# Scaling the even output weight by the gate earlier in the program and keeping the result in DRAM

## The chip, the cores and the metric

The kernel runs on one core of a Trainium2 chip. The metric is the device time of one execution in microseconds (us), as the median of several runs. The engines are named as in the profile: PE is TensorE, DVE is VectorE, ACT is ScalarE, POOL is GpSimd, SP is the engine that issues most DMAs.

## What is computed

Two layers over 1024 tokens of 1024 channels. The even layer runs gated linear attention (GLA, four heads) and multi-head latent attention (MLA, eight heads) in parallel, puts their outputs side by side, multiplies by an output weight, scales each output channel with a gate and adds the result to the residual before a layer norm. The odd layer mixes with a Fourier transform and a gated MLP and ends in the same way.

```python
y_lat = jnp.einsum('bne,ed->bnd', jnp.concatenate([y_gla, y_mla], -1), w_out)   # even layer, w_out 1024 x 1024
x = layer_norm(DEEPNORM_ALPHA * x + gate[:, None, :] * y_lat, post_ln_g[l], post_ln_b[l])
```

The gate multiplies output channels, so it may be multiplied into the columns of the output weight beforehand. `gate` depends on the conditioning vector alone and is known long before the weight is used.

## The kernel before

All arithmetic is float32. A product of two operands is made of three matmuls (`mm3`, lines 143 to 148): each operand is split into a rounded part `hi` (an ACT cast, line 136) and the remainder `lo` (a DVE or POOL subtraction, line 141).

Nearly all large tiles, 128 x 1024 words, come from one pool `big` of 48 buffers through `b4`; tiles of 128 x 512 come from a pool `work` of 8 buffers through `w2`. The tile framework gives out the buffers of a pool in the order in which the program asks for them, sets every semaphore, and fixes the order of each engine's instructions when the program is built, by readiness and then by place in the program. On the chip each engine runs its list in that order.

The order in which the program asks is written by hand with generators: `weave` (line 51) runs several generators side by side, each in proportion to a total that is given with it. The stretch that matters first is woven of three streams: `in_proj_b` (ten projections of 128 columns, the last four of which multiply the GLA outputs by a gate), a chain of `gla` and `mla_ramp`, and the rest of the modulation. `mla_ramp` (line 873) loads and splits the MLA weights, normalised queries and keys, makes the queries and keys of head 0, moves them into place (`mla_prep`, line 978; a row of maxima joins the query tile `qh` by a small POOL DMA of `mr`), and last takes four gate tiles `mg` from DRAM, applies SiLU and writes them back (lines 905 to 909). `mla` (line 1012) then makes the values `V`, and runs eight heads; `attend(hd)` (line 1041) loads a gate tile `mg` for each pair of heads (line 1045), and for each of 20 blocks makes scores `pss`, takes exponentials `pexp` (ACT), splits them into `ph` (ACT cast; the subtraction alternates between DVE and POOL) and multiplies by `V` into `psav`, five blocks behind.

Beside heads 6 and 7 runs `even_pre` (line 1116): it loads the gate of the even layer as a row repeated over 128 partitions (`rowB`), and four row blocks of the output weight (`out_weight`, line 1136: SP load into `owr`, POOL multiplication by the gate, split into `hi` and `lo`). The other four row blocks follow in `rest` of `even_tail` (line 1204), behind the first half of the output projection of three row blocks (`out_proj`, line 1152). The odd layer calls `out_weight` in the same way with its own weight and gate.

Of the kernel before, what the change touches and what calls it, by code (L numbers as in the profile page):

```python
# [63 lines left out]
def chain(*gens):  # L64
    for g in gens:
        yield from g
# [6 lines left out]
def scaled(gen, f):  # L73
    for d in gen:
        yield d * f


def run(g):
    for _ in g:
        pass  # L80
# [1035 lines left out]
def even_pre(k):  # L1116

    nc, A = k.nc, k.A
    k.ow, k.oy = [None] * KD, [[None] * KD, [None] * KD]
    k.ogate = load_rows(k, k.gate[0])  # L1120
    for t in range(4):
        out_weight(k, A["wo0"], t)
        yield 2.5
    yt = []
    for t in range(4):
        x = k.b4(name="yg")
        nc.sync.dma_start(x, k.ygd[t])
        k.D("yg%d" % t, x)
        yt.append(x)
        if t % 2:  # L1130
            split_y(k, yt, t - 1)
            yt = []
        yield 2.5


def out_weight(k, wsrc, j):

    raw = k.b4(name="owr")
    k.nc.sync.dma_start(raw, wsrc[j * P:(j + 1) * P, :])
    k.nc.gpsimd.tensor_tensor(out=raw, in0=raw, in1=k.ogate, op=ALU.mult)  # L1140
    k.ow[j] = k.split(raw, (P, 1024))


# [54 lines left out]
def load_rows(k, src):  # L1198
    t = k.b4(name="rowB")
    k.nc.sync.dma_start(t, src.broadcast_to([P, D]))  # L1200
    return t


def even_tail(k, W):
    nc, A = k.nc, k.A
    k.x1 = [k.dr.tile([P, D], F32, name=f"x1_{i}") for i in range(NT)]

    def rest():
        for t in range(4, KD):
            out_weight(k, A["wo0"], t)  # L1210
        for t in range(0, 4, 2):
            k.D("ym%d" % t, k.mg[t])
            k.D("ym%d" % (t + 1), k.mg[t + 1])
            split_y(k, k.mg[t:t + 2], 4 + t)

    def resid(i):
        x = k.b4(name="xr")
        nc.sync.dma_start(x, A["x"][i * P:(i + 1) * P, :])
        return x

    pend = {}

    def done(i, x, c):
        nc.gpsimd.dma_start(k.x1[i], x)
        k.D("x1_%d" % i, x)
        r, nm = k.ln_stats(x)
        pend[i] = k.b4(name="xn1")
        nc.scalar.activation(out=pend[i], in_=x, func=AF.Identity, scale=r, bias=nm)

    k.h1 = [[], []]  # L1230

    def transposed(hf):
        for j in range(KD):
            if j % 2 == 0:
                hi, lo = k.b4(F32R, (P, 2, 512), name="h1h"), k.b4(F32R, (P, 2, 512), name="h1l")
            ps = k.bank()
            for t in range(4):
                nc.tensor.transpose(ps[:, t * P:(t + 1) * P], pend[4 * hf + t][:, j * P:(j + 1) * P], k.ident)
            hh = k.w2(name="h1")
            nc.scalar.activation(out=hh, in_=ps, func=AF.Identity, scale=k.s1[:, j:j + 1], bias=k.sh1[:, j:j + 1])  # L1240
            k.h1[hf].append(k.split(hh, None, hi=hi[:, j % 2, :], lo=lo[:, j % 2, :], hi_eng="dve"))
            yield 0.65

    first = transposed(0)
    for n, _ in enumerate(out_proj(k, list(range(KD)), rest, 0, resid, done), 1):
        if n in TR0:
            run(itertools.islice(first, TR0[n]))
        if n == WN:
            W.fill(WF)
    return transposed(1)  # L1250
# [41 lines left out]
def odd(k, transposed, W):  # L1292
    nc, A = k.nc, k.A
    T = nc.tensor

    f = [k.b4(F32, (P, 2, 512), name="f") for _ in range(NT // 2)]
    wf = []

    def wnext(c):
        if c == len(wf):  # L1300
            wf.append(W.next())
        return wf[c]

    ev = lambda i, ps: nc.scalar.copy(out=f[i // 2][:, i % 2, :], in_=ps)
    run(weave((natural_steps(k, wnext, 0, ev), 20.8), (chain(lull(TR1[0]), transposed), TR1[0] + TR1[1])))
    odd_consts(k)
    run(natural_steps(k, wnext, 1, ev))
    del wf[:]
    W.fill(2)
    UR, UI = butterflies(k, f)  # L1310
    del f
    X, fr = {}, []

    def dft(stage, g):
        if stage == 0:
            X[g] = dft_tokens(k, [z and z[:, g * P:(g + 1) * P] for z in UR], [z and z[:, g * P:(g + 1) * P] for z in UI])
        else:
            fr.append(dft_channels(k, X.pop(g)))
            k.D("fr%d" % g, fr[-1])


    wv = [W.next() for _ in range(KD // 2)]
    vg = [k.b4(F32, (P, 2, 512), name="vg") for _ in range(NT // 2)]
    mv = k.cpool.tile([P, NT * 4, 2], F32, name="vmv")
    for i in range(NT):
        ps = k.bank()
        o = slice((i % 4) * P, (i % 4) * P + P)
        for kk in range(KD):
            hh = k.h1[i // 4][kk]
            k.mm3(ps, (hh[0][:, o], hh[1][:, o]), (wv[kk // 2][0][:, kk % 2, :], wv[kk // 2][1][:, kk % 2, :]), kk == 0, kk == KD - 1)  # L1330
        for z in DFT.get(i, ()):
            dft(*z)
        v = vg[i // 2][:, i % 2, :]
        k.act(v, ps, AF.Gelu)
        st = k.sm.tile([P, 4, 6], F32, tag="vst", name="vst")
        for g in range(4):
            nc.vector.bn_stats(out=st[:, g, :], in_=v[:, g * P:(g + 1) * P])
            nc.vector.bn_aggr(out=mv[:, i * 4 + g, :], in_=st[:, g, :])
    rs = k.cpool.tile([P, NT * 4], F32, name="vrs")
    for i in range(0, NT, 4):  # L1340
        c = slice(i * 4, i * 4 + 16)
        nc.gpsimd.tensor_scalar(out=rs[:, c], in0=mv[:, c, 1], scalar1=EPS, scalar2=0.0, op0=ALU.add, op1=ALU.add)
        nc.gpsimd.tensor_tensor(out=rs[:, c], in0=rs[:, c], in1=k.mhalf[:, 0:16], op=ALU.pow)
    for i in range(NT):
        for g in range(4):
            c = i * 4 + g
            v = vg[i // 2][:, i % 2, g * P:(g + 1) * P]
            nc.vector.tensor_scalar(out=v, in0=v, scalar1=mv[:, c, 0:1], scalar2=rs[:, c:c + 1], op0=ALU.subtract, op1=ALU.mult)

    gu = []  # L1350
    for t in range(4):
        w = W.next()
        x = k.b4(name="gu")
        proj1(k, w, lambda ps, s: k.act(x[:, s:s + 512], ps, AF.Gelu))
        gu.append(x)

    for t in range(4):
        w = W.next()

        def ev(ps, s):  # L1360
            g = k.w2(name="gs")
            k.act(g, ps, AF.Silu)
            nc.vector.tensor_tensor(out=gu[t][:, s:s + 512], in0=gu[t][:, s:s + 512], in1=g, op=ALU.mult)

        proj1(k, w, ev)
        for s in range(2):
            ps = k.bank("pssgu")
            for c in range(4):
                i = 4 * s + c
                T.matmul(ps[:, c * P:(c + 1) * P], vg[i // 2][:, i % 2, t * P:(t + 1) * P], k.sguw[:, t, :], start=True, stop=True)  # L1370
            sv = k.w2(name="sv")
            bb = k.sgub[:, t:t + 1, :].broadcast_to([P, 4, P])
            nc.vector.tensor_tensor(out=sv.rearrange("p (c x) -> p c x", x=P), in0=ps.rearrange("p (c x) -> p c x", x=P), in1=bb, op=ALU.add)
            o = slice(s * 512, s * 512 + 512)
            nc.vector.tensor_tensor(out=gu[t][:, o], in0=gu[t][:, o], in1=sv, op=ALU.mult)

    k.ow, k.oy = [None] * KD, [[None] * KD, [None] * KD]
    k.ogate = load_rows(k, k.gate[1])
    for t in range(4):
        if t % 2 == 0:  # L1380
            split_y(k, gu[t:t + 2], 4 + t)
        w = W.next()
        out_weight(k, A["wo1"], 4 + t)

        def ev(ps, s):
            g = k.w2(name="gs")
            k.act(g, ps, AF.Silu)
            nc.vector.tensor_tensor(out=fr[t][:, s:s + 512], in0=fr[t][:, s:s + 512], in1=g, op=ALU.mult)

        proj1(k, w, ev)  # L1390
    return fr, gu
# [87 lines left out]
def odd_tail(k, fr):  # L1479
    nc, A = k.nc, k.A  # L1480

    def rest():
        for t in range(4):
            if t % 2 == 0:
                split_y(k, fr[t:t + 2], t)
            out_weight(k, A["wo1"], t)

    def resid(i):
        x = k.b4(name="xr")
        nc.sync.dma_start(x, k.x1[i])  # L1490
        return x

    run(out_proj(k, [4, 5, 6, 7, 0, 1, 2, 3], rest, 1, resid, lambda i, x, c: nc.sync.dma_start(k.out[i * P:(i + 1) * P, c], x[:, c])))
# [3 lines left out]
def hybrid(ctx: ExitStack, tc, A, out, dbg=None):  # L1497
# [11 lines left out]
    h, first = startup(k, context)  # L1509
    ada = ada_rest(k)  # L1510
    in_proj_a(k, h, hc, first, context, W, ada)
    run(weave((in_proj_b(k, h, W), 103.0), (chain(gla(k), scaled(mla_ramp(k), RAMP)), GLA_T + RAMP * 30), (ada, ADA_T)))
    mla(k)
    W = Weights(k, odd_weights(k))
    transposed = even_tail(k, W)
# [98 lines left out]
```

## Time and profile before

| | us |
|---|---|
| median of 3 runs (1150.33 to 1151.75) | 1150.7 |
| the profiled execution, its own time | 1151.5 |
| span of its trace | 1149.0 |
| PE busy | 1093.9 |
| DVE busy | 746.2 |
| ACT busy | 562.7 |
| POOL busy | 261.0 |

The profile is one execution. An engine is busy while it runs an instruction; matmuls are pipelined, so their durations overlap. The granted clock of PE is given as a mean share of full speed. "Idle before" stands in brackets with what ended it. A timeline row merges neighbouring instructions of one line and one tile (x4).

### The profile page before, as it was taken

Reading aid. Unit: us, or ns where it says so; the run is one execution under the profiler, and the core shown is the slowest. Engines: PE = TensorE matmul, PEld = TensorE weight load, DVE = VectorE, ACT = ScalarE, POOL = GpSimd, SP = SyncE. Lnnn points to the kernel's source line nnn. Section 1 sums busy time; section 2 is a strip of 40 time slices with the busy share of each in tenths; the row PEclk is TensorE's granted clock in tenths of the full one; section 3 lists DMA queues with packets and bytes.
Section 4 is the critical chain, followed back from the end, with each engine's and each line's share of the span. In section 5 each row is a group of like instructions: output and inputs, shape, how many; then the busy total and the mean of one; then the engine's idle time right before and its main releaser. Section 6 shows DMA issues by size and latency. Waiting matters only on the chain.

```text
span 1149.0 us, 14553 instructions
## 1 busy us (share of the span) xinstructions
PE 1093.9 (95%) x5288; PEld 868.1 (76%) x5288; DVE 746.2 (65%) x1264; ACT 562.7 (49%) x965; POOL 261.0 (23%) x260
## 2 busy tenths in 40 slices
PE   5889999899999999999999999999999999999997
PEld 3668778688687877767677666888788888888885
DVE  6867694866655675766777677798526633664544
ACT  6285655676562367857777778313422223332000
POOL 3520000000000023433324366343101000122111
PEclk8989999999999999999999999999999999999999
DMA  9635562333535752113302424333400311125111
GB/s 371 244 127 193 205 223 100 135 123 106 197 101 190 227 158 51 27 43 88 70 1 51 124 73 132 126 111 128 165 1 1 110 37 55 56 65 213 53 55 55
DMA packets 41752, 131.89 MB, mean 115 GB/s; under 512 B 5673, under 2 KB 7465, under 8 KB 41682
## 3 DMA queue, kind: packets, MB, share of 16 engines
q1 hardware_dynamic: 35578, 114.77, 30.9%
q0 software_dynamic: 3312, 10.26, 2.2%
q10 hardware_dynamic: 2792, 5.94, 1.3%
q8 instruction: 41, 0.67, 0.2%
q14 instruction: 29, 0.24, 0.1%
HBM read 98.37 MB, written 20.36 MB: 103 GB/s over the span
## 4 chain that ended last, share of the span: by engine, by line
PE 76%; DVE 8%; ACT 6%; issue 3%; POOL 3%; DMA 3%; SPq 0%; POOLq 0%; DVEq 0%; ACTq 0%
PE ps L146 11%; PE ps L148 10%; PE ps L147 10%; PE pso L147 5%; PE pso L146 5%; PE pso L148 5%; PE psm L998 3%; PE pss L1073 3%; PE pss L1074 3%; PE pss L1075 3%; PE psav L1059 2%; PE psav L1057 2%; PE psav L1058 2%; PE psn L146 1%; PE psn L148 1%
## 5 line engine op out<-in xcount | busy, mean ns | idle before, releaser
L141 POOL TENSOR_TENSOR ph<-pexp,ph 128x512 fp32r<-128x512 f32 x80 | 108.3, 1358 | 170.3 <-ACT ph L136 150.4
L118 ACT ACTIVATE pexp<-pss 128x512 f32<-128x512 f32 x160 | 93.3, 596 | 63.8 <-PE pss L1075 60.9
L999 DVE TENSOR_REDUCE mx<-psm 128x1 f32<-128x512 f32 (+1 forms) x192 | 102.2, 593 | 14.1 <-PE psm L998 13.7
L146 PE MATMUL ps<-h,hi 128*128 128x512 f32 x256 | 103.4, 415 | 7.2 <-ACT h L331 3.3
L148 PE MATMUL ps<-h,lo 128*128 128x512 f32 x256 | 103.0, 402 | 3.5 <-DVE lo L308 1.6
L141 DVE TENSOR_TENSOR ph<-pexp,ph 128x512 fp32r<-128x512 f32 x80 | 75.1, 943 | 45.3 <-ACT ph L136 42.9
L147 PE MATMUL ps<-h,hi 128*128 128x512 f32 x256 | 102.1, 399 | 0.8 <-DVE h L332 0.8
L146 PE MATMUL pso<-hi,yh 128*128 128x512 f32 x256 | 99.8, 390 | 0.0
L147 PE MATMUL pso<-lo,yh 128*128 128x512 f32 x256 | 99.7, 390 | 0.0
L141 DVE TENSOR_TENSOR lo<-wraw,hi 128x1024 fp32r<-128x1024 f32 x37 | 47.1, 1283 | 80.4 <-ACT hi L136 75.4
L148 PE MATMUL pso<-hi,yl 128*128 128x512 f32 x256 | 99.0, 389 | 0.0
L136 ACT CAST ph<-pexp 128x512 fp32r<-128x512 f32 x160 | 95.2, 620 | 2.8
L146 PE MATMUL ps<-h1h,hi 128*128 128x512 f32 x192 | 75.2, 391 | 0.0
L147 PE MATMUL ps<-h1l,hi 128*128 128x512 f32 x192 | 74.7, 389 | 0.0
L148 PE MATMUL ps<-h1h,lo 128*128 128x512 f32 x192 | 74.7, 389 | 0.0
L1140 POOL TENSOR_TENSOR owr<-owr,rowB 128x1024 f32<-128x1024 f32 x16 | 43.8, 2752 | 118.8 <-DMA owr<-wo 118.7
L1059 PE MATMUL psav<-ph,V 128*96 128x512 f32 x160 | 64.2, 401 | 1.7 <-POOL ph L141 1.4
L146 PEld LDWEIGHTS ps<-h,hi 128*128 128x128 f32 x256 | 48.8, 192 | 19.8 <-ACT h L331 4.8
L1057 PE MATMUL psav<-ph,V 128*96 128x512 f32 x160 | 63.4, 396 | 0.2
L148 PEld LDWEIGHTS ps<-h,lo 128*128 128x128 f32 x256 | 49.0, 191 | 17.2 <-DVE lo L308 2.8
L147 PEld LDWEIGHTS ps<-h,hi 128*128 128x128 f32 x256 | 49.3, 192 | 10.7 <-DVE h L332 1.4
L148 PEld LDWEIGHTS pso<-hi,yl 128*128 128x128 f32 x256 | 48.1, 188 | 10.1
(364 smaller groups left out, 2615.5 us busy)
## 6 DMA issues: line engine op xcount, KB each, us to landing
aw<-ada SPq DMA_DIRECT2D x32, 512.0 KB, 7.5
araw<-ada SPq DMA_DIRECT2D x32, 512.0 KB, 4.6
wraw<-we SPq DMA_DIRECT2D x16, 512.0 KB, 8.3
owr<-wo SPq DMA_DIRECT2D x16, 512.0 KB, 3.5
xr<-x SPq DMA_DIRECT2D x16, 512.0 KB, 6.4
wraw<-wd SPq DMA_DIRECT2D x12, 512.0 KB, 3.4
xt<-x SPq DMA_DIRECT2D x8, 512.0 KB, 6.1
kt<-kn SPq DMA_DIRECT2D x16, 256.0 KB, 3.6
```

The source lines that it names most:

```text
L118: r = self.nc.scalar.activation(out=out, in_=in_, func=func, **kw)
L136: self.nc.scalar.copy(out=hi, in_=src)
L141: (lo_eng or self.nc.vector).tensor_tensor(out=lo, in0=src, in1=f32(hi), op=ALU.subtract)
L146: t.matmul(out, lhs[0], rhs[0], start=start, stop=False)
L147: t.matmul(out, lhs[0], rhs[1], start=False, stop=False)
L148: t.matmul(out, lhs[1], rhs[0], start=False, stop=stop)
L998: T.matmul(ps[:, :n], q[0][0:96, i * P:(i + 1) * P], cols(kt[0], s, n)[0:96], start=True, stop=True)
L999: nc.vector.reduce_max(out=mx[:, i, b:b + 1], in_=ps[:, :n], axis=AX.X)
L1057: T.matmul(a[0:96, :], vhi(j, hd), hi, start=j == 0, stop=False)
L1059: T.matmul(a[0:96, :], vhi(j, hd), lo, start=False, stop=j == NK - 1)
L1073: T.matmul(ps, kc[0], q[0][:, o], start=True, stop=False)
L1140: k.nc.gpsimd.tensor_tensor(out=raw, in0=raw, in1=k.ogate, op=ALU.mult)
```

## The change

The multiplication of the even output weight by the gate moves from `out_weight` into a new generator `gated_weights`, woven into `mla_ramp` with the ramp's total of 30 against 8. It loads the repeated gate row, and for each of the eight row blocks loads the block (SP), multiplies it in place (POOL), and stores it to a DRAM tile `wog` (a POOL DMA). `out_weight` then loads from `wog` in the even layer and multiplies no more; in the odd layer it gets the gate as an argument and does what it did.

```diff
@@ even_pre
     k.ow, k.oy = [None] * KD, [[None] * KD, [None] * KD]
-    k.ogate = load_rows(k, k.gate[0])
     for t in range(4):
-        out_weight(k, A["wo0"], t)
+        out_weight(k, k.wog, t)
         yield 2.5
@@
+def gated_weights(k):
+    nc, A = k.nc, k.A
+    k.wog = k.spill("wog", D, D)
+    gate = load_rows(k, k.gate[0])
+    for j in range(KD):
+        raw = k.b4(name="owg")
+        nc.sync.dma_start(raw, A["wo0"][j * P:(j + 1) * P, :])
+        nc.gpsimd.tensor_tensor(out=raw, in0=raw, in1=gate, op=ALU.mult)
+        nc.gpsimd.dma_start(k.wog[j * P:(j + 1) * P, :], raw)
+        yield 1.0
+
-def out_weight(k, wsrc, j):
+def out_weight(k, wsrc, j, gate=None):
     raw = k.b4(name="owr")
     k.nc.sync.dma_start(raw, wsrc[j * P:(j + 1) * P, :])
-    k.nc.gpsimd.tensor_tensor(out=raw, in0=raw, in1=k.ogate, op=ALU.mult)
+    if gate is not None:
+        k.nc.gpsimd.tensor_tensor(out=raw, in0=raw, in1=gate, op=ALU.mult)
     k.ow[j] = k.split(raw, (P, 1024))
@@ rest() of even_tail
-            out_weight(k, A["wo0"], t)
+            out_weight(k, k.wog, t)
@@ odd, odd_tail
-        out_weight(k, A["wo1"], 4 + t)
+        out_weight(k, A["wo1"], 4 + t, k.ogate)
@@ hybrid
-    run(weave((in_proj_b(k, h, W), 103.0), (chain(gla(k), scaled(mla_ramp(k), RAMP)), GLA_T + RAMP * 30), (ada, ADA_T)))
+    run(weave((in_proj_b(k, h, W), 103.0), (chain(gla(k), scaled(weave((mla_ramp(k), 30.0), (gated_weights(k), 8.0)), RAMP * 30.0 / 38.0)), GLA_T + RAMP * 30), (ada, ADA_T)))
```

## Rows read from the trace of the kernel before

**Rows 1.** The page: engines' busy time, share of the span, instructions.
```profile
PE 1093.9 (95%) x5288; PEld 868.1 (76%) x5288; DVE 746.2 (65%) x1264; ACT 562.7 (49%) x965; POOL 261.0 (23%) x260
```

**Rows 2.** Busy time by stretch: length, engines, PE clock, DMA share, GB/s.
```profile
450.00:640.00 190.00, 186.00 (x810) 137.60 (x809) 130.21 (x220) 140.84 (x248) 69.83 (x57) 0.99 0.22 53
640.00:710.00 70.00, 65.32 (x264) 44.35 (x263) 53.03 (x61) 53.23 (x96) 39.26 (x24) 0.98 0.35 99
710.00:735.00 25.00, 25.00 (x111) 19.92 (x110) 22.98 (x20) 16.85 (x27) 15.33 (x7) 1.00 0.55 182
...
655.00:660.00 5.00, 5.00 (x17) 3.61 (x15) 4.94 (x9) 4.18 (x8) 1.94 (x1) 0.66 0.01 3
```

**Rows 3.** What PE waited for in 640 to 710: us, times, longest.
```profile
PE pss L1073 <- DVE mx L999: 1.5, 1, 1.5
PE psav L1059 <- POOL ph L141: 1.4, 4, 0.7
PE psm L998 <- DMA qh<-qrh: 0.8, 1, 0.8
```

**Rows 4.** Timelines of SP, POOL, ACT and DVE at head 7's start.
```profile
643.36 0.83 SPq L1200 DMA_DIRECT2D rowB<-gate  x1
...
650.91 2.38 POOL L1140 TENSOR_TENSOR owr<-owr,rowB 128x1024 f32<-128x1024 f32 x1 [8.79 <-DMA owr<-wo]
...
656.42 1.04 ACT L136 CAST hi<-owr 128x1024 fp32r<-128x1024 f32 x1
657.37 4.26 ACT L136 CAST ph<-pexp 128x512 fp32r<-128x512 f32 x8
...
651.15 2.69 DVE L1066 TENSOR_TENSOR rl<-rl,mg 64x512 f32<-64x512 f32 x1 [0.28 <-ACT rl L118]
...
675.98 0.68 DVE L1066 TENSOR_TENSOR rl<-rl,mg 64x512 f32<-64x512 f32 x1 [0.19 <-ACT rl L118]
```

**Rows 5.** The multiplications of 640 to 735 (ns), and POOL's 512 KB store.
```profile
L1140 POOL TENSOR_TENSOR owr<-owr,rowB x8: 2383/2842/3385, 650.9 to 724.2; 128x1024 f32<-128x1024 f32 x8
...
L1224 POOL DMA_DIRECT2D x<-xr x8: 623/623/673, 747.2 to 810.0; - x8
```

**Rows 6.** Busy time by stretch in the ramp, columns as in rows 2.
```profile
299.00:345.00 46.00, 44.34 (x310) 35.69 (x309) 27.95 (x49) 27.68 (x43) 3.25 (x6) 1.00 0.38 129
345.00:380.00 35.00, 32.86 (x138) 26.49 (x137) 20.41 (x28) 12.29 (x19) 1.63 (x3) 0.95 0.48 161
380.00:395.00 15.00, 15.00 (x69) 12.38 (x69) 8.67 (x17) 2.84 (x4) 0.54 (x1) 1.00 0.94 270
395.00:415.00 20.00, 20.00 (x90) 16.18 (x89) 14.26 (x33) 11.19 (x16) 5.40 (x15) 1.00 0.97 297
```

**Rows 7.** SP's timeline at the end of the ramp.
```profile
386.18 1.25 SPq L153 DMA_DIRECT2D wraw<-we  x1
...
390.12 4.67 SPq L907 DMA_DIRECT2D mg<-mgd  x4
...
406.08 0.32 SPq L1045 DMA_DIRECT2D mg<-mgd  x1
...
409.30 1.45 SPq L181 DMA_DIRECT2D qh<-qrh  x1
```

**Rows 8.** Timelines of ACT, DVE and PE: last projection, start of head 0.
```profile
391.68 1.05 ACT L136 CAST hi<-wraw 128x1024 fp32r<-128x1024 f32 x1 [4.71 <-DMA ogr<-ogd]
...
394.64 1.22 DVE L141 TENSOR_TENSOR lo<-wraw,hi 128x1024 fp32r<-128x1024 f32 x1
...
395.91 0.50 PE L148 MATMUL ps<-h,lo 128*128 128x512 f32 x1
...
415.73 0.80 PE L1073 MATMUL pss<-qh,kt 97*128 97x512 f32 x1
...
416.85 0.40 PE L1073 MATMUL pss<-qh,kt 97*128 97x512 f32 x1
...
417.54 0.40 PE L1073 MATMUL pss<-qh,kt 97*128 97x512 f32 x1
```

More of the change, by code (lines that the diff above doesn't have):

```diff
@@ L1485, in rest @@
                 split_y(k, fr[t:t + 2], t)
-            out_weight(k, A["wo1"], t)
+            out_weight(k, A["wo1"], t, k.ogate)
     def resid(i):
```

## The prediction

> **What bounds the kernel now.** I read the page first: PE is busy 1093.9 of 1149.0 us, POOL 261.0 [rows 1]. So the end moves only where PE stops, or runs at the lower clock, and POOL's work counts only where PE waits for it. Next the busy time by stretch, to see where PE stops. In 450 to 640, plain attention, PE is busy 186.0 of 190 us at a mean granted clock of 0.99; in 640 to 710, heads 6 and 7, 65.32 of 70 at 0.98; in 710 to 735, where the other four blocks of the weight are multiplied, 25.00 of 25 [rows 2]. The list of what PE waited for then gives names: 1.5 us for the maxima `mx` on DVE, 1.4 us for `ph` from POOL, 0.8 us for a DMA of head 7's queries [rows 3]. Last the timelines, for why these were late. POOL stood 8.79 us until the first weight block had landed, multiplied until 653.3, and only behind the cast of that block (656.42) did ACT run eight casts of `ph` in one go [rows 4]. The order is the buffers' order: the pool gives out tiles as the program asks, so every `ph` asked for behind `hi` of the weight waits until `hi` can be written. In the same time DVE needed 2.69 us for a product that takes 0.68 at 675.98 [rows 4], and the maxima stood behind it.
>
> **What goes, beside heads 6 and 7.** Four multiplications of 2.84 us (median, of the eight in 640 to 735 [rows 5]), 11.4 us of POOL, and one load of the repeated gate row, of 0.83 us on SP, ahead of the first weight block [rows 4]. The four loads stay. What that is worth I take from the stretch against its neighbour. 640 to 710 loses 70 - 65.32 = 4.7 us to stops and, in 655 to 660 at a clock of 0.66, 5 x 0.34 = 1.7 us to the lower of the two clock levels: 6.4 us. 450 to 640 loses 190 - 186 = 4.0 and, at 0.99, 1.9 us: 5.9 in 190, or 2.2 in 70 us [rows 2]. If the stretch becomes like its neighbour, 6.4 - 2.2 = 4.2 us come back, and what is late next is the DMA of head 7's queries, 0.8 us [rows 3]. The bounds: nothing, if the casts of `ph` still wait as long for the load that stays; and all but the query DMA, 6.4 - 0.8 = 5.6. I take 4.2, because the two largest waits have multiplications as their cause.
>
> The long DVE product began at 651.15 and ended at 653.84, POOL's multiplication ran from 650.91 to 653.29: the product did its 0.68 us after the multiplication [rows 4]. The Trainium skill's page "SBUF — State Buffer", section "SBUF: two separate sides", states this as a rule: VectorE and GpSimd share a pair of SBUF ports under an exclusive lock, held for a whole instruction, against which a VectorE operation with two SBUF inputs blocks while GpSimd reads SBUF. The trace agrees, 2.69 against 0.68, and the rule speaks against the change, since the lock goes where the multiplication goes. If the meetings in the ramp fall where PE doesn't wait, the sum below stays at -2.4; if they fall on its path, it is the +3.3 of the last rival.
>
> **What goes behind the heads.** The other four multiplications, 11.4 us of POOL in 710 to 735. PE is busy all through there [rows 2], with the three row blocks of the first half of the output projection, so I cost their absence at nothing; a gain is excluded because no PE time is idle, and nothing is added that could lose.
>
> **What comes, in the ramp.** Nine more loads on SP (eight blocks, the gate row), eight multiplications and eight stores on POOL. POOL: 8 x (2.84 + 0.62 for the issue of a 512 KB store [rows 5]) = 27.7 us. Over 299 to 415 it is busy 3.25 + 1.63 + 0.54 + 5.40 = 10.8 of 116 us [rows 6], so it has room; behind a waiting multiplication are queued the stores of `ygd` and the small DMA of `mr`, which the first scores wait for. Each multiplication may also hold one DVE operation, as it held the product of 651.15, for up to 2.69 - 0.68 = 2.0 us [rows 4].
>
> Now where they fall. Following the generators by hand, block 0 comes behind the first MLA weight, 1 and 2 around `mla_qr`, 3 within `mla_qk(0)`, and 4 to 7 behind the weight of the last projection, three of them within the maxima of head 0 and all ahead of the four `mg` loads. The first three lie where the DMA engines are busy 0.38 to 0.48; the rest lie in 380 to 415, where they are busy 0.94 to 0.97 [rows 6]. Two places there can cost.
>
> First, the weight of the last projection. Its load is issued at 386.18 [rows 7], ACT casts it as soon as it has landed (391.68), and DVE's `lo` ends at 395.86; the matmul that needs it starts at 395.91 [rows 8]. So there is no cover. Block 3 puts 0.52 MB of load ahead of it, and 380 to 415 moves 270 x 15 + 297 x 20 = 9990 KB in 35 us, 285 GB/s [rows 6]: 1.8 us. Bounds: nothing, if block 3 gets through the less busy stretch ahead, and twice that with its store, 3.6. I take 1.8.
>
> Second, the start of the attention. The four `mg` loads were issued from 390.12 to 394.79, 1.17 us each; `mg` 0 was given SiLU, stored, and loaded again at 406.08, and SP then issued head 1's queries until 410.75 [rows 7]. Buffers are asked for in that order, and the second `ph` of head 0 comes behind them. PE starts its scores at 415.73, and a block of three matmuls takes it 0.69 us (416.85 to 417.54); the pool `work` holds eight exponentials, so 8 x 0.69 = 5.5 us, until 421.2 [rows 8]. A cast takes 0.53 us (eight in 4.26 [rows 4]), and I allow 1.2 for cast and subtraction, so the chain has 421.2 - 1.2 - 410.75 = 9.3 us to spare. What delays it: at least the four issues, 4 x 1.17 = 4.7 us. At most the buffers: the tiles that I count in the code there are 16 of `h`, 14 `hi` and `lo`, two each of `kt`, `kn`, `qn`, `qr`, `q`, and `ckx`, `ktx`, `acc` and the raw weight, 44 of 48, and the gate row and block 3 make 46. Then block 6 waits for a store and `mg` 0 for `h`, which the last projection frees in its second half. The first half ends 24 matmuls of 0.23 us behind 395.91, at 401.4, and block 7 and `mg` 0 need one buffer each, some 1.3 us of matmuls later: about 403, or 13 us behind 390.12 [rows 7, 8]. The two delays lie about the slack of 9.3 us; halfway, 8.9, costs nothing, and that is what I take, with both ends in the range. At the far end it costs 13 - 9.3 = 3.7 us, and 1.7 more for a stretch at the lower clock such as the one at 655 [rows 2].
>
> **The sum.** -4.2 + 1.8 + 0 = -2.4 us. The profiled execution took 1151.5 us (span 1149.0), so 1149.1 on its scale; it stands 0.8 above the median of 1150.7. On the median: 1148.3.
>
> **The rivals.** *No change.* The casts of `ph` wait for the load of the weight instead of its product. The load was issued behind 643.36 + 0.83 and released POOL at 650.9, some 6.7 us, against 2.38 for the multiplication [rows 4]: if the load is most of the wait, half the gain stays, -2.1, and the 1.8 of the ramp takes it: 1150.4. For it speaks that the eight loads are not removed; against it the DVE wait of 1.5 us, the largest, which came behind the product that was held.
>
> *Slower.* The ramp's buffers run out, the `mg` chain comes 13 us later, and the first scores run dry: -4.2 + 1.8 + 3.7 + 1.7 = +3.0, 1153.7. It decides as soon as the second load of `mg` comes later than 406.08 + 9.3 = 415.4. For it speaks the count of 46 of 48 and DMA engines at 0.97; against it that the order of PE is laid out anew with the later buffers in view, so that other work may stand there.
>
> *DVE held in the ramp* is a second way to slower. If two of the eight multiplications meet a `lo` that PE waits for, 2 x 2.0 + 1.7 for the lower clock: -4.2 + 1.8 + 5.7 = +3.3, 1154.0. Against it: DVE is busy 20.41 of 35 and 14.26 of 20 us there [rows 6]. The Trainium skill's page "SBUF — State Buffer" would have every such meeting block in full.
>
> **How the numbers follow.** The forecast, the gain kept and the ramp nearly free: 0.40. No change: 0.30. Slower by the `mg` chain 0.22, by DVE held 0.08. A measurement of this kernel tells about 0.2%, 2.3 us, from no change, so these are the chances of faster, same and slower. The range reaches from 1150.7 - 5.6 = 1145.1, the most that the heads can give back, to 1156.0: that is the slower case with block 3's 3.6 for 1.8 (1155.5), and half a us for the spread of the runs. The ends of all costs together, 1150.7 + 0 + 3.6 + 3.7 + 1.7, are 1159.7; I leave them out. The forecast's own range is 1145.1 to 1148.4.
>
> **What would show it.** Right: in 640 to 710 no L1140 on POOL, the first cast of `hi` at the landing of `owr`, `rl` on DVE at 0.68, PE idle near 2; in the ramp, eight multiplications near 2.8 us, PE idle there as before but for some 2 us behind 390. Wrong: the second load of `mg` issued behind 415, PE idle or at the lower clock in 415 to 430, DVE's `lo` of the last projection ending well behind PE's need, or casts of `ph` still in packs of eight beside head 7. Since every engine's order is laid out anew, stops in stretches that the change doesn't touch may come or go too; one with its lower clock is worth some 3 us, and the PE clock and idle time by stretch would show it.

## The result, and the profile after

The change made the kernel slower: 1158.7 us (median of 5 runs, 1157.9 to 1164.1) against 1150.7; the ratio of the comparison is 1.0097, 95% interval 1.0074 to 1.0120. In a second set of runs it was 1.0090 (1.0067 to 1.0113). The forecast was 1148.3, its range ended at 1156.0.

The profiled execution of after is the slowest of the five: it took 1164.1 us, its span is 1162.2, so its stops are together some 5 us larger than those of the median run. A second trace of the same kernel (span 1160.4) has the same two largest stops of PE in the ramp, for `V` (4.4 us) and for a weight (4.1), so the pattern is read here, and sizes are taken from the timed runs.

Busy time by stretch after (columns as in rows 2). First the ramp and the start of the attention, then three stretches 17 us later than in rows 2, since the heads come that much later:

```profile
299.00:345.00 46.00, 44.57 (x321) 35.98 (x320) 28.18 (x50) 26.02 (x41) 7.28 (x10) 1.00 0.40 141
345.00:380.00 35.00, 31.33 (x125) 24.87 (x124) 21.11 (x24) 10.86 (x15) 7.58 (x7) 0.90 0.67 232
380.00:395.00 15.00, 12.82 (x56) 10.32 (x55) 6.35 (x10) 4.46 (x8) 3.49 (x3) 0.94 0.75 210
395.00:415.00 20.00, 20.00 (x88) 16.30 (x87) 15.15 (x26) 2.24 (x3) 10.16 (x8) 0.96 0.91 307
415.00:430.00 15.00, 8.54 (x35) 6.62 (x34) 3.83 (x11) 8.06 (x11) 7.48 (x16) 0.80 1.00 373
430.00:450.00 20.00, 17.30 (x66) 12.64 (x65) 17.05 (x35) 12.93 (x24) 5.23 (x4) 0.89 0.36 99
467.00:657.00 190.00, 185.99 (x810) 137.83 (x809) 130.60 (x221) 141.07 (x249) 69.47 (x57) 0.99 0.23 53
657.00:727.00 70.00, 66.97 (x284) 47.33 (x284) 47.46 (x66) 59.65 (x107) 31.33 (x23) 1.00 0.38 117
727.00:752.00 25.00, 25.00 (x110) 20.35 (x109) 14.46 (x19) 11.32 (x17) 0.55 (x1) 1.00 0.41 133
```

The two stretches that follow those of [rows 6], in the kernel before:

```profile
415.00:430.00 15.00, 13.79 (x53) 9.90 (x52) 12.88 (x26) 9.33 (x18) 3.87 (x3) 0.89 0.21 50
430.00:450.00 20.00, 20.00 (x90) 15.07 (x89) 12.89 (x24) 15.42 (x28) 5.65 (x6) 1.00 0.01 2
```

Plain attention is unchanged (185.99 of 190, 186.00 before). In 657 to 727 PE loses 3.0 us at full clock, against 6.4 in [rows 2]. The loss lies in the ramp and at the start of the attention: PE stands 3.7 us in 345 to 380 and 2.2 in 380 to 395, against 2.1 and 0 in [rows 6], then 6.5 in 415 to 430, with the clock at 0.80, and 2.7 in 430 to 450, against 1.2 at 0.89 and 0. The stages' first instructions tell the same: the first scores came at 415.7 before [rows 8] and come at 432.5, 16.8 us later, and the first matmul of the odd layer 12.8 us later (817.0 against 804.2). So the ramp costs some 17 us in this execution, and what stands between gives about 4 back.

What PE waited for, first in 299 to 450, then in 657 to 727 (us in total, times, longest):

```profile
PE ps L146 <- DVE Vl L1029: 6.5, 1, 6.5
PE psm L998 <- DMA qh<-qrh: 4.9, 2, 2.7
PE ps L146 <- ACT hi L136: 3.6, 1, 3.6
```
```profile
PE psmt L1005 <- DVE m L1002: 1.4, 1, 1.4
PE psav L1059 <- POOL ph L141: 0.7, 1, 0.7
PE psm L998 <- DMA ql<-qrl: 0.7, 1, 0.7
```

None of the three in the ramp is a wait for a multiplication. To see why each came late, the timelines (start, us) of SP, ACT, PE and DVE:

```profile
361.77 0.42 SPq L153 DMA_DIRECT2D wraw<-we  x1
...
388.03 0.59 SPq L181 DMA_DIRECT2D qh<-qrh  x1
...
393.43 1.98 SPq L153 DMA_DIRECT2D wraw<-we  x1
...
398.96 4.99 SPq L1142 DMA_DIRECT2D owg<-wo  x4
...
410.42 4.75 SPq L907 DMA_DIRECT2D mg<-mgd  x4
425.97 0.32 SPq L1045 DMA_DIRECT2D mg<-mgd  x1
```
```profile
365.29 1.04 ACT L136 CAST hi<-wraw 128x1024 fp32r<-128x1024 f32 x1 [0.67 <-DMA wraw<-we]
...
400.10 1.05 ACT L136 CAST hi<-wraw 128x1024 fp32r<-128x1024 f32 x1 [8.78 <-DMA wraw<-we]
...
416.41 1.06 ACT L118 ACTIVATE mg<-mg 128x1024 f32<-128x1024 f32 x1 [6.44 <-DMA mg<-mgd]
...
425.58 1.06 ACT L118 ACTIVATE mg<-mg 128x1024 f32<-128x1024 f32 x1 [2.43 <-DMA mg<-mgd]
426.55 0.57 ACT L1026 CAST V<-ps 128x512 fp32r<-128x512 f32 x1
```
```profile
428.05 0.77 PE L146 MATMUL ps<-hi,ckx 128*128 128x512 f32 x1 [6.46 <-DVE Vl L1029]
```
```profile
402.38 1.22 DVE L141 TENSOR_TENSOR lo<-wraw,hi 128x1024 fp32r<-128x1024 f32 x1
```

A projection's weight is loaded at 361.77 and cast at 365.29, and PE stood 3.6 us for that cast. The last projection's weight is loaded at 393.43 (before: 386.18 [rows 7]), 7.2 us later. It stands on SP behind the moves of head 0's queries, and these are already 7.0 us late (388.03); before:

```profile
381.07 0.58 SPq L181 DMA_DIRECT2D qh<-qrh  x1
```

From its issue to its cast the weight takes 6.7 us (5.5 in [rows 7, 8]), and its `lo` ends at 403.60, 7.7 us later than in [rows 8], so the last projection goes on 7.7 us later. The four `mg` loads come at 410.42, 20.3 us later than in [rows 7], and the reload 19.9 later. What SP waited for at these loads (us in total, times, longest):

```profile
SPq L907 <- PE ps L148: 5.7, 2, 5.2
SPq L907 <- DMA wog<-owg: 3.0, 1, 3.0
```

The wait of 5.2 us, for a matmul of the last projection, is at the first of the four, the one that is loaded again at 425.97; the wait of 3.0 us, for the store of a block, is at the third. And in ACT's list the casts of `V` stand behind the fourth SiLU of `mg`: that one waited for its load until 425.58, and PE, whose next bank had to wait for a cast of `V`, stood from 421.6 to 428.05. In 421 to 428 the DMA engines are full:

```profile
421.00:428.00 7.00, 0.59 (x3) 0.17 (x1) 0.85 (x3) 3.47 (x5) 1.53 (x6) 0.72 1.03 418
```

Beside the heads (ACT, POOL, DVE at head 7's start, answering to rows 4):

```profile
669.62 1.05 ACT L136 CAST hi<-owr 128x1024 fp32r<-128x1024 f32 x1
...
671.16 3.73 ACT L136 CAST ph<-pexp 128x512 fp32r<-128x512 f32 x7
...
671.84 8.10 POOL L141 TENSOR_TENSOR ph<-pexp,ph 128x512 fp32r<-128x512 f32 x5 [12.15 <-PE psm L998]
...
668.63 0.69 DVE L1066 TENSOR_TENSOR rl<-rl,mg 64x512 f32<-64x512 f32 x1 [0.28 <-ACT rl L118]
```

The held product is back at 0.69 (2.69 in [rows 4]). Seven casts of `ph` still come in one go behind `hi`.

### The profile page after: what moved, and what is told of

Same layout as the page of the kernel before. It is cut to its first block, busy times and chain, and to the rows that moved or that the text cites. A ratio compares the mean times of both kernels' runs of the same rounds, so it can differ in the third digit from the quotient of the medians.

```text
span 1162.2 us, 14604 instructions
## 1 busy us (share of the span) xinstructions
PE 1098.3 (95%) x5288; PEld 872.7 (75%) x5288; DVE 733.3 (63%) x1264; ACT 562.8 (48%) x965; POOL 261.1 (22%) x268
## 4 chain that ended last, share of the span: by engine, by line
PE 59%; DMA 3%; ACT 1%; issue 1%; POOL 1%; DVE 1%; SPq 0%; POOLq 0%; DVEq 0%; ACTq 0%
PE ps L146 6%; PE ps L148 6%; PE ps L147 6%; PE pso L148 5%; PE pso L147 5%; PE pso L146 5%; PE psm L998 3%; PE pss L1073 3%; PE pss L1074 3%; PE pss L1075 3%; PE psav L1059 3%; PE psav L1057 2%; PE psav L1058 2%; PE psn L146 1%; PE psn L148 1%; PE psn L147 1%
## 5 line engine op out<-in xcount | busy, mean ns | idle before, releaser
L146 PE MATMUL ps<-h,hi 128*128 128x512 f32 x256 | 105.5, 424 | 8.4 <-ACT hi L136 3.6
L999 DVE TENSOR_REDUCE mx<-psm 128x1 f32<-128x512 f32 (+1 forms) x192 | 102.4, 593 | 16.2 <-PE psm L998 15.9
L147 PE MATMUL ps<-h,hi 128*128 128x512 f32 x256 | 103.7, 405 | 0.5 <-DVE h L332 0.5
L141 DVE TENSOR_TENSOR ph<-pexp,ph 128x512 fp32r<-128x512 f32 x80 | 68.1, 851 | 48.9 <-ACT ph L136 43.9
L198 POOL TENSOR_SCALAR rstd<-bnmv 128x1 f32<-128x1 f32 x34 | 23.5, 691 | 146.8 <-DVE bnmv L1188 124.2
L147 PEld LDWEIGHTS pso<-lo,yh 128*128 128x128 f32 x256 | 48.1, 188 | 10.1
```

The lines of the kernel that those rows point to most:

```text
L141: (lo_eng or self.nc.vector).tensor_tensor(out=lo, in0=src, in1=f32(hi), op=ALU.subtract)
L146: t.matmul(out, lhs[0], rhs[0], start=start, stop=False)
L147: t.matmul(out, lhs[0], rhs[1], start=False, stop=False)
L999: nc.vector.reduce_max(out=mx[:, i, b:b + 1], in_=ps[:, :n], axis=AX.X)
```

## The experiments

The kernel before was run beside every group; its medians were 1147.4 to 1150.7, so only ratios are compared. A difference of two ratios is turned into us with 1150.7. "Price" is the ratio less that of the first run, which has no step in the ramp; each interval is about 2 us to either side, so prices are good to some 2.5 us.

| run | ratio to before | interval | price, us |
|---|---|---|---|
| gain_alone | 0.9959 | 0.9944 to 0.9974 | 0 |
| early, early_again | 0.9974, 0.9982 | 0.9955 to 0.9992, 0.9966 to 0.9999 | 1.7, 2.6 |
| buffers_only | 1.0003 | 0.9986 to 1.0020 | 5.1 |
| thin | 1.0018 | 1.0001 to 1.0035 | 6.8 |
| load_only | 1.0038 | 1.0024 to 1.0053 | 9.1 |
| blocks03, blocks47 | 1.0045, 1.0055 | 1.0026 to 1.0064, 1.0034 to 1.0075 | 9.9, 11.0 |
| copy_pinned | 1.0050 | 1.0032 to 1.0068 | 10.5 |
| no_mult | 1.0097 | 1.0082 to 1.0112 | 15.9 |
| after, after_again | 1.0097, 1.0090 | 1.0074 to 1.0120, 1.0067 to 1.0113 | 15.9, 15.1 |
| pool_loads | 1.0110 | 1.0090 to 1.0131 | 17.4 |
| behind_mg | 1.0164 | 1.0149 to 1.0179 | 23.6 |

**Gain and cost apart** (gain_alone, ramp_alone). First the changed kernel with nothing in the ramp:

```diff
-        out_weight(k, k.wog, t)
+        out_weight(k, A["wo0"], t)      # in even_pre and in rest
-    ... weave((mla_ramp(k), 30.0), (gated_weights(k), 8.0)) ...
+    ... scaled(mla_ramp(k), RAMP) ...
```


> The changed kernel without the step in the ramp: no block is multiplied or stored, and the last heads load the weight without the gate (so the weight is not scaled, which leaves out part of the computation). It measures what the heads give back. Theory (the heads give back what the stages of the changed kernel's trace show: the head maxima are 17.6 us late, the first block of the layer behind it 12.8): 4.8 us less than before, 1145.9. Rival (the heads gain nothing, the lateness only shrank because work had been put off): 1150.7.

0.9959, or 4.7 us less than before (3.0 to 6.4). Then the kernel before with `gated_weights` woven into the ramp as well, its result unused:

> The kernel before with the step in the ramp added: eight blocks loaded, multiplied and stored there, and the last heads still load, multiply and cast as before. It measures what the ramp costs. Theory (all of the loss is in the ramp, 8.0 + 4.8 us): 12.8 us more than before, 1163.5. Rival (part of the loss is in the last heads, which read the blocks from the new place): 1158.7 or less.

1.0132 (1.0106 to 1.0158), 15.2 us more. Within the intervals the two add up to the result: 15.2 - 4.7 = 10.5 us, or 0.9%. The gain is real, and the loss is the ramp's.

**The multiplications** (no_mult). The line of the POOL multiplication is taken out of `gated_weights`.

> The changed kernel without the eight multiplications in the ramp; loads and stores stay (so the weight is not scaled, which leaves out part of the computation). Theory (the ramp loses by buffers that the blocks hold and by the place of their loads and stores in the queues, not by POOL's arithmetic): a block is held some 2.4 us less, and the time falls by 2 to 3 us only, to about 1156. Rival (the multiplications hold DVE, or POOL's own time delays the stores and the maxima of head 0 behind it): 8 x 2.4 us of POOL go, and the time falls to 1148 to 1150.

The ratio is that of the changed kernel. Eight multiplications (median 2.405 us in the trace of after) cost nothing that can be measured, so neither DVE held by POOL nor POOL's own time is the price. My 2 to 3 us for buffers held less long weren't there either.

**The place** (early, early_again). Only the weave differs:

```diff
-chain(gla(k), scaled(weave((mla_ramp(k), 30.0), (gated_weights(k), 8.0)), RAMP * 30.0 / 38.0))
+chain(weave((gla(k), GLA_T), (gated_weights(k), 8.0)), scaled(mla_ramp(k), RAMP))
```


> The changed kernel with the same loads, multiplications and stores woven with the gated linear attention ahead of the ramp, in place of the ramp. Theory (the ramp loses because its buffers and its queues are full there): nothing stands ahead of the ramp's loads, the first scores come as before at about 416, and the gain of the heads stays: about 1146 to 1148. Rival (eight multiplications and 8 MB of DMA cost wherever they are put, since DVE is held or the stores collide with the weights' loads): 1155 or more.

> The step woven with the gated linear attention, once more with more rounds. Theory (the ramp's place is the price, the gain of the heads stays): 2 to 5 us below before. Rival (the gain seen was scatter): within 1 us of before.

Medians 1145.6 and 1145.75, ratios 0.9974 and 0.9982, both intervals below 1, the second barely: this version beats both kernels, by 2 to 3 us of the 4.7. The same loads, multiplications and stores cost 2 us there and 15 in the ramp. In 150 to 299, where they lie, the DMA engines are busy 0.52 in its trace (0.41 before), and the attention starts as in [rows 8], with the first scores at 415.3. The trace of early_again is of a slower execution (1149.8 us); there they come at 421.5, so the start as before is seen in one of two traces, and the gain rests on the medians.

**Which blocks** (blocks03, blocks47). Half of the blocks is skipped in the loop (`if j >= 4: yield 1.0; continue`, and the reverse).

> The changed kernel with only blocks 0 to 3 scaled and stored in the ramp; blocks 4 to 7 are loaded as they are behind the heads (so half of the weight is not scaled, which leaves out part of the computation). Without any block the kernel took 1144.5, with all eight 1158.7, 14.2 more. Theory (blocks 0 to 3 take buffers from the first loads of the ramp, so that cq, the weight of the gated projection and the moves of head 0 come late; of the 17.6 us by which the maxima of head 1 were late in the trace of the changed kernel, 10.7 stood before the maxima of head 0): 10.7 / 17.6 of 14.2, 8.6 us, so 1153.1. Rival (the four mg loads are what is late, and only blocks 4 to 7 stand ahead of them): 1146 or less.

> The changed kernel with only blocks 4 to 7 scaled and stored in the ramp, where they stand now; blocks 0 to 3 are loaded as they are beside the last heads (so half of the weight is not scaled, which leaves out part of the computation). Theory (blocks 4 to 7 delay the mg loads and the tiles of V behind them, which is 6.9 of the 17.6 us of lateness): 6.9 / 17.6 of 14.2, 5.6 us, so 1150.1, and head 0's maxima come near 408. Rival (the whole price is the mg loads' place): 1157 to 1159.

Each half costs 10 to 11 us. The rival that only blocks 4 to 7 cost fell with blocks03, where the `mg` loads come at 396.24. But the shares that I took from the trace (8.6 and 5.6) were too small for the later half, which came nearer to its rival (12.5 to 14.5 above the kernel without any block): the halves add up to 20.9, more than both together, so part of what each makes late is hidden behind the other. In the traces blocks 0 to 3 move head 0's queries late (386.41 for `qrh`, 381.07 before) and blocks 4 to 7 don't (378.47); they move the `mg` loads late (399.73, 390.12 before).

**Buffers, loads, stores** (buffers_only, load_only). In the first each block's three instructions become `nc.gpsimd.memset(raw[:, 0:8], 0.0)`; in the second only the load stays.

> The changed kernel with no load, no multiplication and no store of the blocks: each block's buffer is asked for at the same place of the program, and POOL writes eight columns of it with a memset (so the weight is not scaled, which leaves out part of the computation; the load of the gate row stays). Theory (the loss is the order in which buffers are given out and the wait for POOL behind the stores of the attention ahead of it): the first half of the loss stays in good part, cq and the weights come late as now, 1149 to 1155. Rival (it is the 8 MB of transfers in a stretch where the DMA engines are full): 1144 to 1146, as without the step.

> The changed kernel with the eight loads in the ramp alone, no multiplication and no store; each buffer comes free as the load lands (the weight is not scaled, which leaves out part of the computation). Theory (buffers held while POOL is waited for): the loads go as buffers come free and hold each only some us, 1146 to 1150. Rival (transfers): half of the bytes, so half of the 14.2 us, 1151 to 1153; and if the loads' place in SP's queue is what costs, all of it, 1157 or more.

Asking for the buffers costs 5.1 us, loads beside that make it 9.1, and with the stores (no_mult) it is 15.9. The theory that the order of the buffers is most of the price fell here: it is a third. load_only lies above its theory and near the half price that its rival, the transfers, gave.

**SP's queue and the order** (pool_loads, behind_mg). The loads go out from POOL's queue; or the blocks stand behind the `mg` loop (`chain(mla_ramp(k), gated_weights(k))`).

> The changed kernel with the eight loads issued from POOL's queue in place of SP's, so that SP never stands at a block's load; buffers are asked for in the same order. Theory (the order of the buffers delays cq, the weights and mg, not SP's queue): no change within 3 us, 6 to 12 us above before. Rival (SP stands at a block's load and holds the moves and weights behind it): 4 us or more better than the changed kernel, so 4 us above before or less.

> The changed kernel with the eight blocks asked for behind the four mg loads, not woven between the loads of the ramp; everything else as it is. Theory (each block ahead of a load of the ramp costs it a buffer): the first loads and head 0's moves come as before, cq at 312 and mg at 390; what is left are the tiles of V and of the attention, which are asked for behind the blocks: 0 to 4 us above before. Rival (eight blocks cost wherever they stand in the ramp): 8 to 11 us above before.

Loads from POOL cost as much as from SP, 17.4 against 15.9, but by another way. On SP two things are on time again: `qrh` is moved at 381.66 and the last projection's weight loaded at 386.52 (381.07 and 386.18 before, 388.03 and 393.43 after). So it is the blocks' loads ahead of them in SP's list that make these two late in after, as the rival had it in part. In their place PE waited 6.4 us for head 0's maxima `mr`, whose DMA stands in POOL's list behind a block that waited for its load; the prediction had named that place:

```profile
PE pss L1073 <- DMA qh<-mr: 6.4, 1, 6.4
```
```profile
421.79 2.34 POOL L1143 TENSOR_TENSOR owg<-owg,rowB 128x1024 f32<-128x1024 f32 x1 [5.37 <-DMA owg<-wo]
424.09 0.59 POOL L181 DMA_DIRECT2D qh<-mr  x1
```

So the run moves the price from one queue to the other, and equal times don't show that SP's queue is without a part in it. The Trainium skill, page "Trainium Kernel Development and Optimization", section "Key Constraints", says that DMAs from the SP, ACT and POOL queues run on the same 16 engines; the trace agrees, since with the loads on POOL's queue these are busy 0.87 in 395 to 415 and 0.91 in 415 to 430, against 0.91 and 1.00 in after. Behind `mg` the price grew to 23.6, against both expectations. What PE waited for there, in 299 to 460, and the end of SP's list:

```profile
PE psm L998 <- DMA qh<-qrh: 14.6, 2, 7.6
PE ps L146 <- DVE Vl L1029: 4.9, 1, 4.9
```
```profile
402.14 7.86 SPq L1142 DMA_DIRECT2D owg<-wo  x4
...
410.53 3.10 SPq L1142 DMA_DIRECT2D owg<-wo  x4
415.25 0.33 SPq L1045 DMA_DIRECT2D mg<-mgd  x1
430.69 0.49 SPq L181 DMA_DIRECT2D qh<-qnh  x1
```

All eight blocks now lie in 402 to 437, and head 1's queries come 22 us later than before (430.69 against 408.71). The other wait of 7.6 us is at head 0's maxima, ahead of every block: PE's list, laid out anew, put them ahead of a projection whose weight was split by 379.05 and which ran from 387.15 only. So a share of each price is the new order of PE, which these runs can't take apart.

**One buffer fewer** (buffers47). The kernel before with `pool("big", 47)` for `pool("big", 48)`:

> The kernel before with 47 buffers of 4 KB in place of 48, nothing else. Theory (the ramp uses the last buffer already, so that each one that a block holds delays a load): the ramp loses, the second load of cq or the weight of the gated projection comes some us later, 1 to 4 us above before. Rival (buffers are no limit there): within 1 us of before.

1.0032 (1.0014 to 1.0051), 3.7 us, in the range of the theory, but not for its reason: the loss lies at another place. Its PE is busy 137.28 of 149 us in 150 to 299 (140.81 before), and as long as before in 299 to 450 (145.95 of 151 against 145.98). In the ramp of this trace one buffer fewer cost nothing.

**Bytes or buffers** (dram_copy, copy_pinned, thin). First the blocks as copies from DRAM to DRAM, without a buffer:

```diff
-        raw = k.b4(name="owg")
-        nc.sync.dma_start(raw, A["wo0"][j * P:(j + 1) * P, :])
-        nc.gpsimd.tensor_tensor(out=raw, in0=raw, in1=gate, op=ALU.mult)
-        nc.gpsimd.dma_start(k.wog[j * P:(j + 1) * P, :], raw)
+        r = slice(j * P, (j + 1) * P)
+        nc.sync.dma_start(k.wog[r, :], A["wo0"][r, :])
+        nc.gpsimd.dma_start(k.wo2[r, :], A["wo0"][r, :])
```


> The changed kernel with no buffer for the blocks: at the place of each load SP copies the block from DRAM to DRAM, at the place of each store POOL does the same again, so 2 x 4.2 MB are moved as now, but no tile of the pool is asked for and nothing waits (the weight is not scaled, which leaves out part of the computation; the gate row's load stays). Theory (buffers held by loads and stores in flight): the ramp costs little, 3 to 5 us less than before. Rival (the transfers themselves, against the weights and moves, in a stretch where the DMA engines are busy 0.94 to 0.97 already): 4 us or more above before.

1.0145 (1.0130 to 1.0160), and no answer: with nothing to wait for, the copies went out at the start of the kernel, as SP's timeline shows.

```profile
1.55 2.71 SPq L1143 DMA_DIRECT2D wog<-wo  x4
17.15 4.37 SPq L1143 DMA_DIRECT2D wog<-wo  x4
...
317.09 0.33 SPq L153 DMA_DIRECT2D wraw<-wuq  x1
```

The first load of the ramp comes 18.2 us later than in before's trace (298.91), and from there to the last score little is lost (405.1 us, 403.4 in gain_alone). So the copies were held at their place: SP's behind the load or move ahead of it, POOL's reading what SP's wrote.

```diff
+        k.order(nc.sync.dma_start(k.wog[r, :], A["wo0"][r, :]), k.sp)   # k.sp: SP's last load or move
+        nc.gpsimd.dma_start(k.wo2[r, :], k.wog[r, :])
```


> As the DRAM to DRAM copies before, but each copy on SP is held behind the load or move that stands ahead of the block's load in the program, and POOL's copy reads what SP's wrote, so that the transfers lie in the ramp and not at the start of the kernel; no buffer is asked for (the weight is not scaled, which leaves out part of the computation). Theory (bytes alone suffice): 5 us or more above before, by late moves and mg loads at 385 to 420. Rival (bytes cost only because a buffer is held until they have landed): 0 to 4 us below before.

And the reverse, everything as it is but for the bytes: `raw[:, :64]`, `gate[:, :64]` and 64 columns of both DRAM tensors in the three instructions.

> The changed kernel with 64 of each block's 1024 columns loaded, multiplied and stored in the ramp (so most of the weight is not scaled, which leaves out part of the computation): the same instructions, places in the queues, buffers and waits, 1/16 of the bytes. Theory by now (the bytes: the step's loads and stores share the DMA engines with the weights, moves and mg loads of the ramp, and hold their buffers for as long as they land): nearly all of the price goes, within 3 us of before. Rival (the buffers' order and the places in the queues cost by themselves): 7 to 11 us above before, as the changed kernel.

> The changed kernel once more, beside the two above, for its ratio on the same chip and a second trace: 8 to 11 us above before.

Bytes without buffers cost 10.5 us, buffers and places with 1/16 of the bytes 6.8, both together 15.1 to 15.9. thin is 2.1 us above before, within the 3 us on record, but before still has the work beside the heads; measured from gain_alone, 6.8 of 15.9 us stay without the bytes, so the theory that the bytes are nearly all of it fell too. Each alone is enough to make the kernel lose its gain, and they nearly add up (17.3). copy_pinned differs in one more thing that no run takes apart: its copies read and write DRAM, where a load or a store does one of the two. Busy time in 395 to 430 of gain_alone, of thin and of copy_pinned (columns as in rows 2), whose reloads of `mg` come at 406.79, 413.29 and 415.26:

```profile
395.00:415.00 20.00, 20.00 (x91) 16.32 (x90) 14.26 (x31) 11.50 (x17) 5.39 (x15) 1.00 0.99 319
415.00:430.00 15.00, 13.75 (x57) 9.55 (x56) 13.68 (x28) 9.86 (x19) 3.96 (x3) 1.00 0.24 62
```
```profile
395.00:415.00 20.00, 19.80 (x89) 15.63 (x87) 12.29 (x24) 7.13 (x10) 8.85 (x23) 1.00 0.71 252
415.00:430.00 15.00, 11.27 (x33) 7.83 (x34) 12.36 (x30) 11.03 (x21) 3.02 (x2) 0.81 0.67 192
```
```profile
395.00:415.00 20.00, 19.49 (x89) 15.77 (x88) 12.69 (x24) 4.08 (x5) 4.54 (x9) 1.00 0.97 381
415.00:430.00 15.00, 11.22 (x33) 6.95 (x32) 7.68 (x21) 11.46 (x20) 2.90 (x10) 0.77 0.83 254
```

In gain_alone the DMA engines are busy only 0.24 in 415 to 430, and PE runs on at full clock. In thin the DMA engines have room in 395 to 415 (0.71): the chain is late because its loads are issued late, the `mg` loads from 401.60, behind a wait of 4.0 us that the list of SP's waits puts down to POOL's multiplication of a block. In copy_pinned the loads are issued early, from 395.30, but 381 GB/s pass in 395 to 415 and they land late (16.1 us in the median of its `mg` loads, against 7.0 in thin).

## Why the prediction was wrong

**The heads: right.** -4.2 was forecast, -4.7 (-6.4 to -3.0) was measured by itself. The held product went from 2.69 to 0.69 us. What is late next is not the DMA of head 7's queries alone (0.7): the longest wait, 1.4 us, is for the row maxima `m` on DVE. One sign named as wrong did appear, the pack of casts of `ph` (7 for 8); but PE waited only 0.7 us for `ph` in the stretch, so the pack comes without the multiplication too, and it costs little. The loads of the blocks stay in gain_alone, so they were not most of the wait, as the rival "no change" had it; the multiplications and the load of the gate row, which went together, were. The other four multiplications cost nothing, as said: PE is busy 25.00 of 25 in 727 to 752.

**The ramp: the term that was mis-sized.** The sum gave it 1.8 + 0 us; ramp_alone measured 15.2. Three steps made it so.

**Blocks 0 to 2: costed at nothing, the step that failed first.** They lie where the DMA engines are half idle, but blocks03 shows 9.9 us for blocks 0 to 3. With the blocks' loads ahead of them in SP's list, head 0's queries go out 7.0 us late and the weight of the last projection 7.2; with these loads on POOL's queue both are on time (pool_loads), and with 1/16 of the bytes they are 2.0 and 2.3 late (thin). The price for block 3's bytes ahead of that weight, 1.8, was near: from issue to cast it took 1.2 us longer. What the sum lacked is that the weight would be issued late. The other late weight, for which PE waited 3.6 us, was loaded at 361.77 after and at 350.54 before. buffers_only has it late too (360.86), with none of the blocks' bytes moved, and so has blocks47 (357.20), where only the gate row stands ahead of it; no run has the gate row alone.

**The `mg` chain: right in kind, counted from too early, and slack on one path only.** The first `mg` load was to wait, at most, for a tile of `h` that the last projection frees in its second half, 13 us late. It did wait for that matmul, 5.2 us, but the projection itself was 7.7 us late: 13 + 7.7 = 20.7, measured 20.3. The waits for a block's store (3.0 us) came behind it, at the third load, and kept the fourth SiLU late. The slack of 9.3 us was worked out for the second `ph`. But PE stopped earlier, for `V`: its casts stand in ACT's list behind the SiLU of `mg`. The text named what is queued behind the waiting instructions on POOL, and not on ACT. So "halfway, 8.9, costs nothing" failed at both ends. That PE's stop goes by way of ACT's list is read from the trace; no run changed that order.

**The bytes: one transfer of ten priced.** The rows showed the DMA engines at 0.94 to 0.97 in 380 to 415 [rows 6], and the text itself put blocks 3 to 7 there. That is five loads and five stores: ten times 1.8, 18 us as an estimate from those rows, if nothing were hidden; the sum had one of them. The transfers of all eight blocks alone cost 10.5 (copy_pinned). In 380 to 430 the trace of after moves 14.9 MB, before's 10.7.

**The rivals.** *Slower by the `mg` chain* had the right sign, and its condition, a second `mg` load later than 415.4, was met at 425.97. Its price of 3.7 + 1.7 was too small: PE's stop for `V` alone is 6.5 us in this execution. Nor does its threshold part cheap from dear: thin and blocks47 reload earlier, at 413.29 and 413.95, and pay 6.8 and 11.0, since the ramp loses by the other ways too. Over all of 299 to 450 PE stands 11.4 us longer than before (busy 134.6 us for 146.0); the lower clock, estimated as 1 less the mean clock times the length over the six stretches, takes up to 10.4 us for 3.4 (idle time is counted in, so the two overlap). *DVE held in the ramp* was not it: without the multiplications the ratio stays. The exclusive lock of the Trainium skill's page "SBUF — State Buffer", section "SBUF: two separate sides", is seen where it went, beside head 7 (2.69 to 0.69 us); in the ramp no run shows it on PE's path. The text left the end of all its costs, 1159.7, out of the range. That it would have held the 1158.7 is luck: it takes the gain of the heads as nothing.

**What stays open.** How much of each price is the new order of PE's list. Every kernel here has its own, and in behind_mg it has a part in a single wait of 7.6 us. Open too are the share of the gate row, and how the price divides between buffers, places in SP's and POOL's queues, and bytes: the runs show that each of them costs, not that they add.

## What to carry to other kernels

Work moved out of a busy stretch has to be priced by every byte and every buffer that it takes at its new place: here 8.4 MB of loads and stores and eight short-lived buffers cost 15 us just ahead of the attention, and 2 us one stage earlier. Before calling a delay slack, follow every list in which the delayed instruction stands, and not only its own chain of data, and count the delay from where its start will lie after the change. Room on the DMA engines is not enough: blocks 0 to 3 alone cost 9.9 us, and three of them lie where these were half idle, but in the queue ahead of loads that PE was about to need.

## What the runs showed of the hardware

The same POOL multiplication, 128x1024 with both inputs in SBUF, took 2.405 us in the median in the ramp (2.368 to 2.837) against 2.842 beside and behind the last heads [rows 5]. Copies from DRAM to DRAM landed in 6.5 us (SP) and 6.3 (POOL) for 512 KB in the ramp, about as long as the loads and stores that they stood for (6.6 and 6.7). After a stop of 3.6 us the granted clock was 0.57 in 365 to 372, so much of that stretch ran at the lower of the two levels.
